# A mixture-of-experts router that works on batches of token tiles instead of one tile at a time

## The chip, the cores and the metric

The kernel runs on one core of a Trainium2 chip. The core has a matrix engine (TensorE, PE in the profile), a vector engine (VectorE, DVE), a scalar engine (ScalarE, ACT), GpSimd (POOL), and SP (SyncE), which here issues nearly all DMA transfers. The metric is the device time in microseconds (us), the median of several runs; lower is better.

## The reference

Two layers of a diffusion backbone work on 512 latent tokens and 256 context tokens of width 1024. Each layer mixes tokens in four groups of heads, projects the result back with w_out and adds it to the stream with a gate, and then runs a mixture of experts:

```python
def moe_ffn(h, wg, bg, we, be, w_gate, w_up, w_down):
    lg = hf @ wg + bg                                  # 4 groups
    pg = softmax(lg)
    g_sel = argmax(lg)
    p_sel = pg[g_sel]
    le = (hf @ we + be).reshape(T, 4, 8)               # 8 experts in each group
    top_v, top_i = top_k(le[g_sel], 2)
    wts = softmax(top_v) * p_sel
    eid = g_sel * 8 + top_i
    ...
    # for each expert e: the rows sent to it
    y = (silu(x @ w_gate[e]) * (x @ w_up[e])) @ w_down[e]
    # out[token] += weight * y
```

h is the normed and modulated stream: each row of x is scaled by the inverse root of its mean square, then by (1 + scale) and gain, and a shift is added. All of it is float32. Layer 0 routes 768 tokens, layer 1 only the 512 latent ones. There are 32 experts, each with 6 MB of weights.

## The kernel before

A tile here is 128 tokens. Layer 0 has nt = 6 tiles (four latent, two context), layer 1 has nt = 4. The code is written as a program in order; a scheduler then sets the order of the instructions on each engine, so instructions of neighbouring tiles may be interleaved on an engine, but each engine, and SP's queue of transfers, works strictly in the order that it was given.

**The end of the output projection.** For each of four column blocks c (256 columns) and each tile t, 24 matmuls (L1787; three products of high and low parts, eight each) fill a PSUM bank, VectorE multiplies it by the gate (L1790) and GpSimd adds it to the tile x1[t] (L1791). In the last block (c == 3) the router is woven in, LAG = 2 tiles behind.

**token_tile(t)** (L1751). SP stores x1[t] as the start of the accumulator (L1753). TensorE transposes the tile into PSUM in eight parts (L1757), ScalarE sums its squares and copies the transposed tile to hTt (L1759), and TensorE makes 36 logits from it (L1762, 16 instructions in the trace). row_rs (L1165) and small_rsqrt (L1149) turn the sum of squares into the row scale rs by nine small VectorE instructions (L1171, L1154, L1155, and L1158 and L1162 three times). VectorE scales the tile (L1768), GpSimd adds the shift (L1769), SP stores h2 (L1770). The logits are scaled and biased by L1772. At t == 0 and t == 4 new modulation rows are loaded first (bc_row, L1766); their buffers and PSUM's two-bank tags allow one set at a time.

**Router.tile(t, lg)** (L897) finds the group maximum, masks the other groups, finds the best and second-best expert by first_max (L886: a maximum, a mask times an index table, a minimum, a mask), and makes the two weights. It counts rows for the same expert in earlier tokens with two small matmuls (L922, L923), splits the weights into three bf16 parts (L926, L928), and for each of the two choices makes EV, a mask times six values (L932), the row's rank R (L933), and for two blocks of 64 slots a 0/1 selection S (L936), which a matmul adds into the tables L (L937). Where an operand is one number per row, these instructions take it as a scalar operand. Most scratch tags have two buffers.

**finish() and table()** (L940, L951) read L for each of the two blocks (L956) and make gather indices, scatter indices and weights, by about a dozen instructions on 32 columns a block.

**The experts.** moe() (L1057) gathers the rows of each expert from the stored h2 (L990, GpSimd), runs up (L1012) and down (L1039) projections and scatters the results (L1052). Expert weights come in chunks of 1 MB, six an expert, by fetch() (L1378), each held back until the fifth before it has landed (FLIGHT = 5). Some chunks are asked for early: FIRST = 12 in layer 0 and 16 in layer 1 ahead of the experts, of which 4 and 7 before the output projection (EARLY). Their places are those that other tiles have left: the sides of the output projection's weights, and in layer 1 also scratch of the router. The chunks up to the eighteenth wait for the second gather, "tokens before more weights".

Of the kernel before, what the change touches and what calls it, by code (L numbers as in the profile page):

```python
# [18 lines left out]
P = 128  # L19
# [165 lines left out]
def bcast(ap, *shape):  # L185
    return ap.to_broadcast(list(shape))
# [678 lines left out]
class Router:  # L865
# [20 lines left out]
    def first_max(self, v, w, iota, tag):  # L886

        E, nc = self.E, self.E.nc
        m, i = E.t(tag + "m", 1, bufs=2), E.t(tag + "i", 1, bufs=2)
        e = E.t(tag + "e", w, bufs=2)  # L890
        nc.vector.reduce_max(m, v, axis=AX)
        nc.vector.scalar_tensor_tensor(e, v, m, iota, op0=ALU.is_equal, op1=ALU.mult)  # L892
        nc.vector.tensor_reduce(i, e, axis=AX, op=ALU.min)
        nc.vector.tensor_scalar(e, iota, i, None, op0=ALU.is_equal)  # L894
        return e, m

    def tile(self, t, lg):  # L897

        E, nc = self.E, self.E.nc
        io4, io32 = E.c["miota"][:, :4], E.c["miota"][:, 4:36]  # L900
        G, gm = self.first_max(lg[:, :4], 4, io4, "rg")
        sm = E.t("rsm", 8, bufs=2)
        ex, lm = E.t("rex", 4, bufs=2), E.t("rlm", [4, 8], bufs=2)
        nc.vector.tensor_scalar(sm[:, 0:1], gm, -1.0, None, op0=ALU.mult)
        nc.scalar.activation(ex, lg[:, :4], AF.Exp, bias=sm[:, 0:1], accum_out=sm[:, 1:2])
        nc.vector.tensor_scalar(G, G, -1.0, 1.0e30, op0=ALU.add, op1=ALU.mult)
        nc.vector.tensor_tensor(lm, lg[:, 4:36].rearrange("p (g e) -> p g e", g=4), bcast(G.unsqueeze(2), P, 4, 8), op=ALU.add)
        lm = lm.rearrange("p g e -> p (g e)")
# [3 lines left out]
        nc.scalar.activation(sm[:, 2:3], v1, AF.Exp, scale=-1.0, bias=v2)  # L912
        nc.vector.scalar_tensor_tensor(sm[:, 3:4], sm[:, 2:3], 1.0, sm[:, 1:2], op0=ALU.add, op1=ALU.mult)
        w = sm[:, 4:6]
        nc.vector.reciprocal(w[:, 0:1], sm[:, 3:4])
        nc.vector.tensor_mul(w[:, 1:2], w[:, 0:1], sm[:, 2:3])

        Ab = E.t("rA", 32, BF16, bufs=2)
        nc.vector.tensor_add(Ab, E1, E2)
        nc.vector.tensor_add(self.seen[:, t + 1], self.seen[:, t], Ab)  # L920
        rk = E.p1()[:, :32]
        nc.tensor.matmul(rk, E.c["before_b"], Ab, start=True, stop=False, skip_group_check=True)  # L922
        nc.tensor.matmul(rk, E.c["ones_b"], self.seen[:, t], start=False, stop=True, skip_group_check=True)  # L923
        v = self.vals[:, :, t]
        for part in range(3):
            nc.vector.tensor_copy(v[:, :, 2 + part], w)  # L926
            if part < 2:
                nc.vector.tensor_sub(w, w, v[:, :, 2 + part])  # L928
        tmp = E.t("rtmp", 32, bufs=2)
        for k, Ek in enumerate((E1, E2)):  # L930
            R, EV = self.R[:, k, t:t + 1], self.EV[:, k, t]
            nc.vector.tensor_tensor(EV, bcast(Ek.unsqueeze(1), P, 6, 32), bcast(v[:, k].unsqueeze(2), P, 6, 32), op=ALU.mult)  # L932
            nc.vector.tensor_tensor_reduce(tmp, Ek, rk, 1.0, 0.0, op0=ALU.mult, op1=ALU.add, accum_out=R)  # L933
            for b in range(2):
                S = E.t("rS", 128, BF16, bufs=4)
                nc.vector.tensor_scalar(S, self.slots, float(b * NSLOT), R, op0=ALU.add, op1=ALU.is_equal)  # L936
                nc.tensor.matmul(self.L[:, b * 512:b * 512 + 192], S, EV.rearrange("p v e -> p (v e)"),  # L937
                                 start=(t == 0 and k == 0), stop=(t == self.nt - 1 and k == 1), skip_group_check=True)

    def finish(self):  # L940

        E, nc = self.E, self.E.nc
        tables = [self.table(self.L[:, b * 512:b * 512 + 192], 32, self.keep, f"s{b}") for b in range(2)]
        c = E.p1()[:, :32]
        nc.tensor.matmul(c, E.c["ones_b"], self.seen[:, self.nt], start=True, stop=True)
        nc.vector.tensor_copy(self.cnt, c)
        nc.vector.reduce_max(self.most, c, axis=AX)
        nc.vector.tensor_copy(self.top, self.most)
        return tables

    def table(self, L, ne, keep, tag):  # L951


        E, nc = self.E, self.E.nc
        Ls, f = E.t(tag + "Ls", [6, ne], bufs=1), E.t(tag + "f", [2, ne], bufs=1)
        nc.vector.tensor_copy(Ls, L.rearrange("p (v e) -> p v e", v=6))  # L956
        w = keep.t(tag + "w", [2, ne], F32, 1, P)
        gi, si = keep.t(tag + "gi", ne, I32, 1, P), keep.t(tag + "si", ne, I32, 1, P)
        pc = E.c["mpc"]
        nc.vector.scalar_tensor_tensor(f[:, 0], Ls[:, 1], 128.0, Ls[:, 0], op0=ALU.mult, op1=ALU.add)  # L960
        nc.vector.tensor_scalar(f[:, 0], f[:, 0], 2.0, pc[:, 0:1], op0=ALU.mult, op1=ALU.add)
        nc.vector.tensor_copy(gi, f[:, 0])
        nc.vector.tensor_scalar(f[:, 1], Ls[:, 5], -1.0, 1.0, op0=ALU.mult, op1=ALU.add)
        nc.vector.scalar_tensor_tensor(f[:, 1], f[:, 1], pc[:, 1:2], f[:, 0], op0=ALU.mult, op1=ALU.add)
        nc.vector.tensor_copy(si, f[:, 1])
        nc.vector.tensor_add(w[:, 0], Ls[:, 2], Ls[:, 3])
        nc.vector.tensor_add(w[:, 0], w[:, 0], Ls[:, 4])
        if self.nt * 128 > NLAT:
            nc.vector.scalar_tensor_tensor(w[:, 1], Ls[:, 1], NLAT / 128 - 0.5, w[:, 0], op0=ALU.is_gt, op1=ALU.mult)
            nc.vector.tensor_sub(w[:, 0], w[:, 0], w[:, 1])  # L970
        return gi, si, w

    def later(self, e, off):

        E, nc = self.E, self.E.nc
        L = E.p1()[:, :6]
        n = 2 * self.nt
        for i in range(n):
            k, t = i // self.nt, i % self.nt
            S = E.t("rS", 128, BF16, bufs=4)  # L980
            nc.vector.tensor_scalar(S, self.slots, off, self.R[:, k, t:t + 1], op0=ALU.add, op1=ALU.is_equal)
            nc.tensor.matmul(L, S, self.EV[:, k, t, :, e], start=(i == 0), stop=(i == n - 1), skip_group_check=True)
        return self.table(L, 1, E.cur, "sb")
# [181 lines left out]
def row_rs(E, x, tag):  # L1165

    nc = E.nc
    rs = E.t(tag, 1, bufs=2)
    junk = E.t(tag + "j", DM, BF16, bufs=1)
    nc.scalar.activation(junk, x, AF.Square, accum_out=rs)  # L1170
    nc.vector.tensor_scalar(rs, rs, 1.0 / DM, EPS, op0=ALU.mult, op1=ALU.add)  # L1171
    small_rsqrt(E, rs, tag)
    return rs


# [168 lines left out]
ARENA = 49536 - SIDE  # L1344
# [10 lines left out]
LAG = 2  # L1355
AHEAD = 1
# [41 lines left out]
def half_rows(a, t):  # L1398

    return a[t * 256:(t + 1) * 256].rearrange("(p a) c -> p (a c)", a=2)  # L1400


def trunk(tc, d, out):
# [7 lines left out]
    with ExitStack() as top:  # L1411
# [90 lines left out]
        for l in range(2):  # L1502
# [248 lines left out]
            def token_tile(t):  # L1751
# [15 lines left out]
                h2 = E.t("h2", DM, bufs=2)  # L1767
                nc.vector.scalar_tensor_tensor(h2, x1[t], rs, mod[0], op0=ALU.mult, op1=ALU.mult)  # L1768
                nc.gpsimd.tensor_add(h2, h2, mod[1])  # L1769
                nc.sync.dma_start(half_rows(h2d[l], t), h2)  # L1770
                lg = E.t("rlg", 36, bufs=2)
                nc.vector.scalar_tensor_tensor(lg, ps[:, :36], rs, cb[v], op0=ALU.mult, op1=ALU.add)  # L1772
                return lg

            mod, logits = [], []
            for c in range(4):
# [3 lines left out]
                for t in range(nt + LAG * (c == 3)):  # L1780
# [168 lines left out]
```

## Time and profile before

| | |
|---|---|
| median of 3 runs | 2420.07 us (2411.84 to 2425.87) |
| the profiled execution | 2419.79 us, its span 2418.0 us |
| granted TensorE clock, mean | 0.956 |
| TensorE busy | 84% of the span |
| VectorE busy | 41% |
| ScalarE busy | 24% |
| GpSimd busy | 22% |
| DMA from HBM | 554.17 MB, 244 GB/s over the span |
| first gathers | 812.19 us (layer 0) and 1911.46 us (layer 1) from the span's start |

The span runs from the first to the last instruction; the profiled execution's own time has 1.8 us around it. Shares of busy time are means over stages with different limits, so a change in one stage is read from rows of that stage. In the rows, PE is TensorE, DVE VectorE, ACT ScalarE, POOL GpSimd and SPq SP's queue; "out<-in" are the program's names; "arena" and "side" are the two pools of on-chip memory from which nearly all tiles come. A clock of 1.00 is 2.4 GHz, 0.50 is 1.2 GHz. A releaser behind "<-" is the work whose end let the waiting instruction go.

### The profile page before, as it was taken

How to read it: one execution, taken by the hardware profiler on the slowest of the kernel's cores; microseconds unless marked ns; L12 is line 12 of the kernel's file. 1: busy time of each engine (PE TensorE's matmuls, PEld its weight loads, DVE VectorE, ACT ScalarE, POOL GpSimd, SP SyncE). 2: the span in 40 equal slices, each digit the busy share in tenths (PEclk: the TensorE clock that was granted, in tenths of full speed). 3: DMA queues.
4: the chain of work that ended last, by engine and by line, in shares of the span. 5: the costliest groups of instructions: out<-in, count | busy, mean ns of one | idle time of the engine just before them, and what ended most of it. 6: DMA issues, size and time to landing. Idle time of an engine off the chain costs nothing. (4 is left out here: it accounts for less than half of the span.)

```text
span 2418.0 us, 32200 instructions
## 1 busy us (share of the span) xinstructions
PE 2039.0 (84%) x11540; PEld 1186.2 (49%) x11540; DVE 999.4 (41%) x2435; ACT 573.2 (24%) x1138; POOL 537.2 (22%) x429
## 2 busy tenths in 40 slices
PE   5789999999999598887777598999899598877775
PEld 1458778766688333322222386686669333222221
DVE  6751865537746522221112437645584511111110
ACT  4433431344622100000000234314352100000000
POOL 1653413211013122211111225131102221111111
PEclk9999999999998699999999799999999699999998
DMA  6434524202244899999999425420233899999996
GB/s 242 165 116 176 194 105 147 81 9 69 85 143 142 299 378 387 405 401 404 400 395 411 173 92 175 147 103 18 86 126 133 313 393 410 409 408 409 410 403 258
DMA packets 139311, 581.54 MB, mean 241 GB/s; under 512 B 23984, under 2 KB 47873, under 8 KB 88630
## 3 DMA queue, kind: packets, MB, share of 16 engines
q1 hardware_dynamic: 124054, 555.89, 59.5%
q0 software_dynamic: 15008, 22.36, 3.9%
q8 instruction: 152, 2.49, 0.4%
q14 instruction: 97, 0.79, 0.1%
HBM read 554.17 MB, written 36.80 MB: 244 GB/s over the span
## 5 line engine op out<-in xcount | busy, mean ns | idle before, releaser
L1012 PE MATMUL pb<-side,arena 128*64 128x512 f32 x1224 | 288.9, 604 | 45.9 <-DMA side<-in_w_moe 42.2
L1016 DVE COPY arena<-pb 128x512 f32<-128x512 f32 x67 | 46.3, 691 | 501.5 <-PE pb L1012 501.5
L1012 PE MATMUL pb<-arena 128*64 128x512 f32 x920 | 217.9, 605 | 41.8 <-DMA arena<-in_w_moe 38.2
L1028 ACT ACTIVATE arena<-pb 128x256 f32<-128x256 f32 x67 | 25.7, 383 | 902.9 <-PE pb L1025 902.9
L1276 POOL TENSOR_TENSOR wl<-side,wh 128x1024 fp32r<-128x1024 f32 x52 | 125.4, 2412 | 395.5 <-ACT wh L1275 267.1
L1012 PEld LDWEIGHTS pb<-side,arena 128*64 128x64 f32 x1224 | 81.4, 137 | 246.5 <-issue 126.4
L1300 PE MATMUL pw<-hh,wh 128*128 128x512 f32 (+1 forms) x720 | 168.6, 366 | 3.1 <-DVE arena L495 1.9
L1300 PE MATMUL pw<-hh,wl 128*128 128x512 f32 (+1 forms) x720 | 160.5, 358 | 0.0
L1043 DVE SCALAR_TENSOR_TENSOR arena<-pb,arena 128x512 f32<-128x512 f32 x67 | 50.3, 750 | 263.2 <-PE pb L1039 254.5
L1039 PE MATMUL pb<-side,arena 128*64 128x512 f32 x576 | 137.8, 617 | 24.9 <-DVE arena L1029 20.4
L1300 PE MATMUL pw<-hl,wh 128*128 128x512 f32 (+1 forms) x720 | 158.2, 355 | 0.0
L1012 PEld LDWEIGHTS pb<-arena 128*64 128x64 f32 x920 | 62.2, 138 | 190.8 <-issue 96.0
L1052 POOL DMA_INDIRECT acc<-arena x35 | 55.2, 1577 | 387.8 <-DVE arena L1047 338.5
L1300 PEld LDWEIGHTS pw<-hh,wh 128*128 128x128 f32 x720 | 117.8, 190 | 36.1 <-issue 14.4
L1039 PE MATMUL pb<-arena 128*64 128x512 f32 x496 | 115.5, 599 | 21.3 <-DVE arena L1029 20.8
L1300 PEld LDWEIGHTS pw<-hh,wl 128*128 128x128 f32 x720 | 117.9, 189 | 25.1 <-issue 9.9
L1300 PEld LDWEIGHTS pw<-hl,wh 128*128 128x128 f32 x720 | 117.4, 189 | 24.4 <-issue 8.7
L1052 POOL DMA_INDIRECT out_dram<-arena x32 | 50.9, 1590 | 311.4 <-DVE arena L1043 297.2
L990 POOL DMA_INDIRECT arena<-h2d,arena x67 | 69.8, 1042 | 187.5 <-issue 56.0
L1791 POOL TENSOR_TENSOR arena<-arena 128x256 f32<-128x256 f32 x40 | 31.2, 782 | 292.2 <-DVE arena L1790 278.2
L1025 PE MATMUL pb<-ident,arena 128*128 128x128 f32 x268 | 42.4, 280 | 55.4 <-DVE arena L1016 55.4
L1039 PEld LDWEIGHTS pb<-side,arena 128*64 128x64 f32 x576 | 39.0, 140 | 101.5 <-issue 60.8
(367 smaller groups left out, 3444.2 us busy)
## 6 DMA issues: line engine op xcount, KB each, us to landing
side<-in_w_moe SPq DMA_DIRECT2D x215, 1024.0 KB
arena<-in_w_moe SPq DMA_DIRECT2D x169, 1024.0 KB
arena<-in_w_ada SPq DMA_DIRECT2D x53, 512.0 KB
side<-in_w_in SPq DMA_DIRECT2D x52, 512.0 KB
side<-in_w_ada SPq DMA_DIRECT2D x43, 512.0 KB
arena<-in_w_out SPq DMA_DIRECT2D x16, 512.0 KB
arena<-in_x SPq DMA_DIRECT2D x12, 512.0 KB
spd<-arena SPq DMA_DIRECT2D x23, 256.0 KB
```

The lines of the kernel that those rows point to most:

```text
L990: E.gathered = nc.gpsimd.indirect_dma_start(out=xg, out_offset=None, in_=h2d, in_offset=bass.IndirectOffsetOnAxis(ap=gi, axis=0), **(dict( ...
L1012: nc.tensor.matmul(pg[64 * s:64 * s + 64], xT[:, j // 4, j % 4, :], W[j // 2][:, (j % 2) * 1024 + s * 512:(j % 2) * 1024 + s * 512 + 512], ...
L1016: nc.vector.tensor_copy(gu, pg)
L1025: nc.tensor.transpose(pt[:, c * 128:(c + 1) * 128], gu[:, c * 128:(c + 1) * 128], E.c["ident"])
L1028: nc.scalar.activation(hT, pv[:, :, 0, :], AF.Silu)
L1039: nc.tensor.matmul(pd[64 * s:64 * s + 64], hT[:, c, :], W[4 + c // 2][:, (c % 2) * 1024 + s * 512:(c % 2) * 1024 + s * 512 + 512], start=( ...
L1043: nc.vector.scalar_tensor_tensor(y, pd, w[0], g2[0], op0=ALU.mult, op1=ALU.mult)
L1052: E.nc.gpsimd.indirect_dma_start(out=acc, out_offset=bass.IndirectOffsetOnAxis(ap=si, axis=0), in_=y, in_offset=None, compute_op=ALU.add, ...
L1276: (nc.vector if k % 2 else nc.gpsimd).tensor_sub(lo, src, hi.bitcast(F32))
L1300: nc.tensor.matmul(ps[:, :n], w[:, j, :], h[:, j, a:a + n], start=(i == 0), stop=(i == 23))
L1791: nc.gpsimd.tensor_add(x1[t][:, cc], x1[t][:, cc], tmp)
```

## The change

The router works on batches of tiles: in layer 0 on tiles 0 to 3 and then on 4 and 5, in layer 1 on 0 and 1 and then on 2 and 3. token_tile(t, i) keeps the transposes, the sum of squares and the logits, which go to the i-th part of one PSUM bank. After a batch's last tile, token_batch(t0, n) makes the row scales of the n tiles together, the logits, then the n h2 tiles one after the other, and Router.tiles(t0, lg) does the routing with a further dimension of n. Operands of one number per row and tile are now broadcast along the free dimension, so several instructions with a scalar operand become a tensor_tensor, and some fused ones become two. Most scratch tags have one buffer that holds four tiles. finish() makes both tables by one call. The order of the code behind the batch's logits is row scales, logits, modulation rows, h2, routing.

```diff
     def first_max(self, v, w, iota, tag):
...
+        m, i = E.t(tag + "m", 4, bufs=1)[:, :n], E.t(tag + "i", 4, bufs=1)[:, :n]
+        e = E.t(tag + "e", [4, w], bufs=1)[:, :n]
+        wide = lambda a: bcast(a.unsqueeze(2), P, n, w)
+        row = bcast(iota.unsqueeze(1), P, n, w)
         nc.vector.reduce_max(m, v, axis=AX)
-        nc.vector.scalar_tensor_tensor(e, v, m, iota, op0=ALU.is_equal, op1=ALU.mult)
+        nc.vector.tensor_tensor(e, v, wide(m), op=ALU.is_equal)
+        nc.vector.tensor_tensor(e, e, row, op=ALU.mult)
         nc.vector.tensor_reduce(i, e, axis=AX, op=ALU.min)
-        nc.vector.tensor_scalar(e, iota, i, None, op0=ALU.is_equal)
+        nc.vector.tensor_tensor(e, row, wide(i), op=ALU.is_equal)
         return e, m
 
-    def tile(self, t, lg):
+    def tiles(self, t0, lg):
...
+        G, gm = self.first_max(lg[:, :, :4], 4, io4, "rg")
+        sm = E.t("rsm", [4, 4], bufs=2)[:, :, :n]
+        ex, lm = E.t("rex", [4, 4], bufs=2)[:, :n], E.t("rlm", [4, 32], bufs=1)[:, :n]
+        nc.vector.tensor_tensor(ex, lg[:, :, :4], bcast(gm.unsqueeze(2), P, n, 4), op=ALU.subtract)
+        nc.scalar.activation(ex, ex, AF.Exp)
         nc.vector.tensor_scalar(G, G, -1.0, 1.0e30, op0=ALU.add, op1=ALU.mult)
...
         E1, v1 = self.first_max(lm, 32, io32, "r1")
         nc.vector.scalar_tensor_tensor(lm, E1, -1.0e31, lm, op0=ALU.mult, op1=ALU.add)
         E2, v2 = self.first_max(lm, 32, io32, "r2")
...
+        nc.vector.tensor_sub(sm[:, 0], v2, v1)
+        nc.scalar.activation(sm[:, 0], sm[:, 0], AF.Exp)
+        Ab = E.t("rA", [4, 32], BF16, bufs=1)[:, :n]
         nc.vector.tensor_add(Ab, E1, E2)
...
+        rk = E.p1()[:, :n * 32].rearrange("p (n e) -> p n e", e=32)
+        for i in range(n):
+            nc.vector.tensor_add(self.seen[:, t0 + i + 1], self.seen[:, t0 + i], Ab[:, i])
+            nc.tensor.matmul(rk[:, i], E.c["before_b"], Ab[:, i], start=True, stop=False, skip_group_check=True)
+            nc.tensor.matmul(rk[:, i], E.c["ones_b"], self.seen[:, t0 + i], start=False, stop=True, skip_group_check=True)
+        nc.vector.tensor_reduce(sm[:, 1], ex, axis=AX, op=ALU.add)
...
         for k, Ek in enumerate((E1, E2)):
...
-            for b in range(2):
-                S = E.t("rS", 128, BF16, bufs=4)
-                nc.vector.tensor_scalar(S, self.slots, float(b * NSLOT), R, op0=ALU.add, op1=ALU.is_equal)
...
+            nc.vector.tensor_tensor(self.EV[:, k, tt], bcast(Ek.unsqueeze(2), P, n, 6, 32),
+                                    bcast(v[:, k].unsqueeze(3), P, n, 6, 32), op=ALU.mult)
+        for k, Ek in enumerate((E1, E2)):
+            nc.vector.tensor_tensor(Ek, Ek, rk, op=ALU.mult)
+            nc.vector.tensor_reduce(self.R[:, k, tt], Ek, axis=AX, op=ALU.add)
+        R1 = E.t("rR1", [2, 4], bufs=2)[:, :, :n]
+        nc.vector.tensor_scalar(R1, self.R[:, :, tt], -float(NSLOT), None, op0=ALU.add)
+        for k in range(2):
+            for b, R in enumerate((self.R[:, :, tt], R1)):
+                S = E.t("rS", [4, 128], BF16, bufs=2)[:, :n]
+                nc.vector.tensor_tensor(S, bcast(self.slots.unsqueeze(1), P, n, 128),
+                                        bcast(R[:, k].unsqueeze(2), P, n, 128), op=ALU.is_equal)
+                for i in range(n):
+                    nc.tensor.matmul(self.L[:, b * 512:b * 512 + 192], S[:, i],
...
     def finish(self):
...
-        tables = [self.table(self.L[:, b * 512:b * 512 + 192], 32, self.keep, f"s{b}") for b in range(2)]
+        gi, si, w = self.table(self.L.rearrange("p (b c) -> p b c", b=2)[:, :, :192], 2, 32, self.keep, "s")
...
-ARENA = 49536 - SIDE
+ARENA = 49664 - SIDE
...
+BATCHES = (((0, 4), (4, 2)), ((0, 2), (2, 2)))
...
-            def token_tile(t):
+            def token_tile(t, i):
...
-                rs = row_rs(E, x1[t], "rs2")
+                if i == 0:
+                    batch[:] = [E.p1()[:, :144].rearrange("p (n e) -> p n e", e=36), E.t("rs2", 4, bufs=2)]
+                nc.scalar.activation(E.t("xoj", DM, BF16, bufs=1), x1[t], AF.Square, accum_out=batch[1][:, i:i + 1])
                 nc.scalar.copy(hTt, pt.rearrange("p (j t) -> p j t", j=8))
...
+            def token_batch(t0, n):
+
+                v = t0 // 4
+                ps, rs = batch[0][:, :n], batch[1][:, :n]
+                nc.vector.tensor_scalar(rs, rs, 1.0 / DM, EPS, op0=ALU.mult, op1=ALU.add)
+                small_rsqrt(E, rs, "rs2", n)
+                lg = E.t("rlg", [4, 36], bufs=1)[:, :n]
+                nc.vector.tensor_tensor(lg, ps, bcast(rs.unsqueeze(2), P, n, 36), op=ALU.mult)
+                nc.vector.tensor_tensor(lg, lg, bcast(cb[v].unsqueeze(1), P, n, 36), op=ALU.add)
+                if t0 % 4 == 0:
                     n2 = E.load("h2", d[f"n2g{l}"], bufs=2)
                     mod[:] = [bc_row(v, 4, "rsc", 1), bc_row(v, 3, "rsh", 1)]
                     nc.vector.scalar_tensor_tensor(mod[0], mod[0], 1.0, n2, op0=ALU.add, op1=ALU.mult)
...
+                for i in range(n):
+                    h2 = E.t("h2", DM, bufs=2)
+                    nc.vector.scalar_tensor_tensor(h2, x1[t0 + i], rs[:, i:i + 1], mod[0], op0=ALU.mult, op1=ALU.mult)
+                    nc.gpsimd.tensor_add(h2, h2, mod[1])
+                    nc.sync.dma_start(half_rows(h2d[l], t0 + i), h2)
+                rt.tiles(t0, lg)
...
                     if c == 3 and t >= LAG:
-                        logits.append(token_tile(t - LAG))
-                        if t > LAG:
-                            rt.tile(t - LAG - 1, logits[t - LAG - 1])
-            rt.tile(nt - 1, logits[-1])
+                        t0, n = [b for b in batches if b[0] <= t - LAG][-1]
+                        token_tile(t - LAG, t - LAG - t0)
+                        if t - LAG == t0 + n - 1:
+                            token_batch(t0, n)
```

## Rows read from the trace of the kernel before

**Rows 1.** View by windows, both router stages: busy us (instructions), clock, DMA share, GB/s.

```profile
771.00:812.20 41.20, 23.77 (x132) 20.35 (x130) 36.72 (x228) 8.84 (x21) 7.74 (x5) 0.58 0.79 278
815.00:825.00 10.00, 6.32 (x18) 2.23 (x20) 0.00 (x0) 0.58 (x1) 3.90 (x4) 0.50 0.75 228
1877.00:1890.00 13.00, 6.21 (x30) 5.58 (x31) 12.90 (x67) 3.99 (x10) 3.09 (x2) 0.50 0.83 272
1890.00:1911.50 21.50, 12.32 (x59) 10.39 (x59) 14.64 (x119) 2.42 (x8) 2.38 (x2) 0.50 0.91 352
1911.50:1925.00 13.50, 7.65 (x22) 2.72 (x24) 0.13 (x2) 0.58 (x1) 4.93 (x5) 0.53 0.84 294
2025.00:2125.00 100.00, 83.25 (x392) 29.27 (x390) 13.04 (x21) 6.78 (x14) 18.42 (x14) 1.00 1.02 409
```

**Rows 2.** Timeline of SP's queue around both gathers: start, us, line, transfer, count.

```profile
799.29 3.08 SPq L1378 DMA_DIRECT2D side<-in_w_moe  x5
820.57 1.42 SPq L1378 DMA_DIRECT2D side<-in_w_moe  x2
...
1893.02 3.83 SPq L1378 DMA_DIRECT2D side<-in_w_moe  x5
1908.53 7.36 SPq L1378 DMA_DIRECT2D arena<-in_w_moe  x3
```

**Rows 3.** Waits of SP's queue, first stage, then second: total us, times, longest us.

```profile
SPq L1770 <- POOL arena L1769: 35.5, 6, 14.4
SPq L1378 <- DMA arena<-h2d,arena: 6.7, 1, 6.7
...
SPq L1378 <- DVE arena L932: 11.5, 1, 11.5
```

**Rows 4.** VectorE groups by form, first router stage: busy us, mean ns.

```profile
L1768 DVE SCALAR_TENSOR_TENSOR arena<-arena 128x1024 f32<-128x1024 f32 x6 | 7.7, 1280 | 0.2
L936 DVE TENSOR_SCALAR arena<-miota,arena 128x128 bf16<-128x128 f32 x24 | 6.3, 278 | 0.0
L892 DVE SCALAR_TENSOR_TENSOR arena<-arena,miota 128x4 f32<-128x4 f32 x6 | 5.4, 893 | 0.0
L932 DVE TENSOR_TENSOR arena<-arena 128x192 bf16<-128x192 f32 x12 | 4.3, 397 | 0.0
```

**Rows 5.** GpSimd group by form, same stage.

```profile
L1769 POOL TENSOR_TENSOR arena<-arena 128x1024 f32<-128x1024 f32 x6 | 14.2, 2365 | 28.7 <-DVE arena L1768 23.6 <-DVE arena L916 3.3 <-PE pa L1757 1.7
```

**Rows 6.** VectorE timeline: two dependent instructions of one tile.

```profile
760.11 0.19 DVE L907 TENSOR_TENSOR arena<-arena 128x32 f32<-128x32 f32 x1
760.34 0.19 DVE L891 TENSOR_REDUCE arena<-arena 128x1 f32<-128x32 f32 x1
```

**Rows 7.** View by windows, VectorE alone.

```profile
747.25:809.40 62.15, 57.11 (x290) 0.69 0.63 226
801.04:809.35 8.31, 8.22 (x68) 0.50 1.02 382
1864.57:1908.70 44.13, 36.70 (x193) 0.63 0.75 282
```

**Rows 8.** TensorE timeline, first stage: end of a projection, transposes, one tile's logits.

```profile
755.02 1.12 PE L1787 MATMUL pw<-woh,ol 128*128 128x256 f32 x8
755.98 1.03 PE L1757 MATMUL pa<-ident,arena 128*128 128x128 f32 x8
760.86 3.63 PE L1762 MATMUL pb<-arena 128*128 128x36 f32 x16 [2.65 <-ACT arena L1759]
```

**Rows 9.** Timeline from the tables' first instruction to the first gather, first layer.

```profile
809.87 0.62 DVE L956 COPY arena<-pa 128x192 f32<-128x192 f32 x2 [0.34 <-PE pa L937]
...
812.19 1.25 POOL L990 DMA_INDIRECT arena<-h2d,arena  x1 [13.30 <-DVE arena L948]
```

**Rows 10.** Timeline, second layer: one tile's last projection to its row scale.

```profile
1862.12 0.42 DVE L1790 TENSOR_TENSOR arena<-pw,arena 128x256 f32<-128x256 f32 x1 [2.46 <-PE pw L1787]
...
1864.57 0.15 DVE L1171 TENSOR_SCALAR arena<-arena 128x1 f32<-128x1 f32 x1 [2.03 <-ACT arena L1170]
```

More of the change, by code (lines that the diff above doesn't have):

```diff
@@ L906, in tile @@
         nc.vector.tensor_scalar(G, G, -1.0, 1.0e30, op0=ALU.add, op1=ALU.mult)
[L907 to L908 removed]
+        nc.vector.tensor_tensor(lm.rearrange("p n (g e) -> p n g e", g=4),
+                                lg[:, :, 4:36].rearrange("p n (g e) -> p n g e", g=4),
+                                bcast(G.unsqueeze(3), P, n, 4, 8), op=ALU.add)
@@ new lines, in tiles @@
+        for k, Ek in enumerate((E1, E2)):
[10 more added lines that the diff above has]
+                    nc.tensor.matmul(self.L[:, b * 512:b * 512 + 192], S[:, i],
+                                     self.EV[:, k, t0 + i].rearrange("p v e -> p (v e)"),
+                                     start=(t0 + i == 0 and k == 0), stop=(t0 + i == self.nt - 1 and k == 1),
+                                     skip_group_check=True)
@@ L948, in finish, with table @@
         nc.vector.tensor_copy(self.top, self.most)
-        return tables
-    def table(self, L, ne, keep, tag):
+        return [(gi[:, b], si[:, b], w[:, :, b]) for b in range(2)]
+    def table(self, L, nb, ne, keep, tag):
         E, nc = self.E, self.E.nc
[L955 to L958, printed above, removed]
+        Ls, f = E.t(tag + "Ls", [nb, 6, ne], bufs=1), E.t(tag + "f", [2, nb, ne], bufs=1)
+        nc.vector.tensor_copy(Ls.rearrange("p b v e -> p b (v e)"), L)
+        w = keep.t(tag + "w", [2, nb, ne], F32, 1, P)
+        gi, si = keep.t(tag + "gi", [nb, ne], I32, 1, P), keep.t(tag + "si", [nb, ne], I32, 1, P)
         pc = E.c["mpc"]
-        nc.vector.scalar_tensor_tensor(f[:, 0], Ls[:, 1], 128.0, Ls[:, 0], op0=ALU.mult, op1=ALU.add)
+        nc.vector.scalar_tensor_tensor(f[:, 0], Ls[:, :, 1], 128.0, Ls[:, :, 0], op0=ALU.mult, op1=ALU.add)
         nc.vector.tensor_scalar(f[:, 0], f[:, 0], 2.0, pc[:, 0:1], op0=ALU.mult, op1=ALU.add)
         nc.vector.tensor_copy(gi, f[:, 0])
-        nc.vector.tensor_scalar(f[:, 1], Ls[:, 5], -1.0, 1.0, op0=ALU.mult, op1=ALU.add)
+        nc.vector.tensor_scalar(f[:, 1], Ls[:, :, 5], -1.0, 1.0, op0=ALU.mult, op1=ALU.add)
         nc.vector.scalar_tensor_tensor(f[:, 1], f[:, 1], pc[:, 1:2], f[:, 0], op0=ALU.mult, op1=ALU.add)
         nc.vector.tensor_copy(si, f[:, 1])
-        nc.vector.tensor_add(w[:, 0], Ls[:, 2], Ls[:, 3])
-        nc.vector.tensor_add(w[:, 0], w[:, 0], Ls[:, 4])
+        nc.vector.tensor_add(w[:, 0], Ls[:, :, 2], Ls[:, :, 3])
+        nc.vector.tensor_add(w[:, 0], w[:, 0], Ls[:, :, 4])
         if self.nt * 128 > NLAT:
-            nc.vector.scalar_tensor_tensor(w[:, 1], Ls[:, 1], NLAT / 128 - 0.5, w[:, 0], op0=ALU.is_gt, op1=ALU.mult)
+            nc.vector.scalar_tensor_tensor(w[:, 1], Ls[:, :, 1], NLAT / 128 - 0.5, w[:, 0], op0=ALU.is_gt, op1=ALU.mult)
             nc.vector.tensor_sub(w[:, 0], w[:, 0], w[:, 1])
@@ L1766, in token_tile @@
                     nc.vector.scalar_tensor_tensor(mod[0], mod[0], 1.0, n2, op0=ALU.add, op1=ALU.mult)
[L1767 to L1775, printed above, removed]
+                for i in range(n):
[4 more added lines that the diff above has]
+                rt.tiles(t0, lg)
+            mod, batch = [], []
+            batches = BATCHES[l]
             for c in range(4):
```

56 lines of the change are left out of this document (15 added, 41 removed).

## The prediction

> **What bounds the kernel now.** The place to begin is the window view of an expert phase: in 100 us of it the DMA engines are busy throughout at 409 GB/s while TensorE is only 83% busy (2025 to 2125) [rows 1]. So each expert phase lasts as long as its 192 weight chunks of 1 MB take, counted from the moment the stream runs without holes. The router matters only through that moment. The reader should see three holes ahead of it: DMA share 0.79 from 771 to 812.2 and 0.75 in the ten us after that in layer 0; 0.83, 0.91 and 0.84 from 1877 to 1925 in layer 1 [rows 1]. As idle time that is 41.2 x 0.21 + 10 x 0.25 = 11.2 us and 13 x 0.17 + 21.5 x 0.09 + 13.5 x 0.16 = 6.3 us. Together, 17.5 us, they are about all that a sooner router can win.
>
> Next, SP's queue and its waits say what ends each hole. In layer 0 five weight chunks leave at 799.29, behind h2 stores for which SP stood still (14.4 us once, for GpSimd's addition); the next leave at 820.57, after a 6.7 us wait for the gathered tokens [rows 2, 3]. That is 8.4 us behind the first gather at 812.19 [rows 9]. In layer 1 the same five leave at 1893.02, and the ninth of its nine at 1908.53 after an 11.5 us wait for VectorE, because its place in the arena is the router's own scratch [rows 2, 3]. So the end of the router releases weights directly.
>
> Then, what sets the end of the router: VectorE alone has 57.1 us of work in 62.2 us, and 36.7 in 44.1 [rows 7]. TensorE waits for it by way of ScalarE (2.65 us before one tile's logits) and falls to the low clock (3.63 us for 16 small matmuls) [rows 8]; its mean clock is 0.58 after 771 [rows 1].
>
> **The change, on VectorE.** Counting the code, a tile now issues 44 small VectorE instructions (9 for the row scale, 1 logits, 34 in tile()). A batch of n tiles issues 55 + n: first_max grows from 4 to 5, the row scale from 9 to 12, logits from 1 to 2. Layer 0 goes from 264 to 59 + 57 = 116, layer 1 from 176 to 114. But the work removed was cheap: tiles were interleaved, and 68 instructions of two tiles took 8.31 us, 0.122 each [rows 7]. One tile's dependent instructions start 0.23 us apart [rows 6]. In the change most scratch buffers of a batch have one copy, so the second batch can't pass its first expert maximum until the first has used its E1. I therefore cost the new router as a chain at 0.23 us a step, plus 1.1 ns for each element beyond 32 ((1.28 - 0.19) us over 992 elements, L1768 against L907 [rows 4, 6]).
>
> For n = 2: 6 steps on groups at 0.20; 16 on 32 experts at 0.25; the count matmuls with nine weight instructions above them 1.4; two EV products of 384 elements 0.9; rank and offset 0.9; four selections of 256 elements at 0.33 (1.3). Sum 9.7 us. For n = 4 the same steps: 1.3 + 5.4 + 1.6 + 1.8 + 1.2 + 2.4 = 13.7, say 13.5 as a few overlap. Row scale: 12 x 0.19 = 2.3. Bounds: fully interleaved like the old code (0.122 each plus the longer operands, 1.1 ns x 4,224 and 1,408 elements), row scale included, 11.8 and 8.5 in place of 15.8 and 12.0; with nothing of the second batch in the gaps, 2.0 more a layer. I take the chain, since the single copies force it.
>
> The selections and products with a broadcast operand don't occur in this form before; L932, a product with two broadcast operands (0.40 us for 192 elements), and L936 (0.28 for 128) are nearest [rows 4]. The Trainium skill's page "VectorE: DVE Perf Modes", section "The perf-mode tier table", gives fp32 tensor_scalar twice the rate of tensor_tensor, which speaks against swapping L936's form for the broadcast one; at the faster rate the four selections would take some 1.1 us less for n = 4 and 0.6 for n = 2. L936's 0.28 us against 0.30 by the slope hardly tells the two apart.
>
> **What stays.** Each tile still needs its h2 multiplication (1.28 us) and GpSimd's addition behind it (2.37) [rows 4, 5]. While that addition runs, one VectorE instruction stands: L892 on four elements averages 0.89 us [rows 4]. So a tile costs VectorE up to 3.65 us, before and after, here in a row of four.
>
> **What moves.** VectorE's router work may start only when a whole batch has its squares. In layer 1 a tile's scale begins 2.45 us after its last projection is read out [rows 10]; a projection takes 3 x 0.96 = 2.88 [rows 8], so the scale of tiles 0 and 1 begins at 1862.12 + 2.88 + 2.45 = 1867.5 in place of 1864.6. In layer 0 the fourth tile's projection ends at 756.0 [rows 8] and the scale begins at 758.6 in place of 747.3 [rows 7]: 11 us in which VectorE has little to do. That is the price of a batch of four. On TensorE, ScalarE's copies no longer queue behind an exponential of each tile, so batch 0's logits come near 773 (two projections and three tiles of transposes and logits after 756, at the high clock) to 780 (at the low one).
>
> **Layer 0 in order.** Scale 758.6 to 760.9; four h2 tiles, 14.6 plus 0.8 for h2's two buffers, to 776.3; batch 0's chain to 789.8 (logits are there); the context rows' product and two h2 tiles, 1.2 + 7.3, to 798.3; batch 1's chain less its first 2.0 us, done in gaps, to 806.0. Before: 809.35 [rows 7]. **Layer 1:** scale to 1869.8, two h2 tiles to 1877.1, chain to 1886.8, two h2 tiles to 1894.1, 7.7 more to 1901.8; before 1908.7 [rows 7].
>
> The joint tables take one copy and the three instructions up to the first gather, about 1.5 us in place of 2.3 [rows 9]: 0.8 a layer, bounds 0 and 1.2. First gathers so come 4.2 and 7.8 us sooner.
>
> **What of it reaches the end.** Layer 0: all 4.2, since the five chunks in front need 5.2 MB / 409 GB/s = 12.8 us and are in by 812 to 815, ahead of 820.6 - 4.2. Layer 1: the eight chunks before the ninth leave hardly sooner, as they stand behind the same stores; what the earlier ninth chunk can fill is the idle share from 1890 to 1925, 4.1 us. Sum 8.3 us. The profiled execution took 2419.8, the median of the runs is 2420.1: **2411.5 us**. The shorter instruction list, PSUM held by a batch, and 128 more arena columns I cost at nothing: TensorE and SP have idle time beside them; were the PSUM bank to hold up tile 4's logits, it would cost 3.6 us of TensorE, still ahead of batch 1's turn on VectorE.
>
> **Rivals.** (1) *Throughput, not the chain, decides.* Gaps are filled as now: layer 0 then needs 11.8 + 8.5 + 23.9 from 758.6, ending at 802.8, layer 1 17.0 + 14.6 + 0.8 from 1867.5, ending at 1899.9; with the tables 7.3 and 9.6 us, and if SP lets the side chunks go as much sooner, all of it arrives: 2403. For it: VectorE held 0.122 us an instruction [rows 7]. Against: the single copies. The same page, section "Rules for kernel authors", advises cutting the number of VectorE operations because each pays its pipe's flush; rows 7 against rows 6 show that independent ones here pay about half.
>
> (2) *No gain arrives.* The context's two modulation rows can be loaded only after batch 0's last addition (776.3), behind up to five weight chunks (12.8 us); h2 of tiles 4 and 5 and the last store then end where they do now, and the gather needs every store. 2419.
>
> (3) *The weight stream waits behind the stores; slower.* SP takes its transfers in order, and stores now come in pairs at the end of a batch. If all eight side chunks queue behind the last store, they need 20.5 us after it. That decides from a last store at 800 in layer 0 (820.6 - 20.5) and 1888 in layer 1 (1908.5 - 20.5). With stores at 806, after batch 1's chain, and at 1894: 6.3 + 6.4 us later; with layer 1's behind its chain too, 20 in all: 2432 to 2440, I take 2434. For it: SP already lost 14.4 us so [rows 3]. Against: three chunks slipped between stores before.
>
> **Chances.** Forecast 0.42, (1) 0.30, (2) 0.14, (3) 0.14. A measurement here tells 0.5% from no change, 12.1 us, so faster means below 2408 and slower above 2432. Faster: nine tenths of (1) and a sixth of the forecast, 0.34. Slower: most of (3), 0.13. Same: 0.53. Range: from 2396, rival (1) less the half-spread of the runs shown, to 2428, half of (3); the forecast's own is 2404 to 2418. Some 0.16 lies outside.
>
> **What would show it.** Right: about 116 and 114 small instructions, VectorE's steps 0.2 to 0.3 us apart within a batch, first gathers 4 and 8 us sooner counted from the last projection, and the same 409 GB/s afterwards. Wrong: steps near 0.12 (rival 1); the last h2 store no sooner (2); a longer line of weight issues straight after it, and DMA share under 0.7 ahead of the gather (3). A clock that stays high up to the experts would break the forecast upwards too.

## The result, and the profile after

The changed kernel takes 2438.30 us (median of 7 runs, 2435.16 to 2443.64) where the kernel before takes 2418.11 beside it: ratio 1.0096, 95% interval 1.0081 to 1.0111. It is 20 us above the kernel before; forecast were 2411.5 us and a range up to 2428. The profiled execution has a span of 2434.0 us against 2418.0.

I cut each span at two marks of each layer: the readout of tile 0's last projection block (L1790 before, L1809 after; 744.79 and 1862.12 before, 741.83 and 1863.94 after) and the first gather. The changed kernel reached the first mark 2.96 us sooner, which I put down to chance: in the runs of this document that mark lies between 738.1 and 747.3. From there, layer 0 takes 1122.1 us in place of 1117.3 up to layer 1's mark (first gather after 70.5 in place of 67.4), and layer 1 takes 570.1 in place of 555.9 (first gather after 63.5 in place of 49.3): -2.96 + 4.8 + 14.2 = 16.0, the whole difference. Behind layer 1's gather both kernels need the same 506.5 us. Of the 19.0 us lost behind the first mark, 14.2 are thus lost in the router stage of layer 1, and 4.8 between layer 0's mark and layer 1's.

The first view is that of VectorE alone in the two stretches from mark to gather (us, busy and instructions, clock, DMA share, GB/s), of the changed kernel; the second the same of the kernel before.

```profile
741.83:812.35 70.52, 43.05 (x143) 0.74 0.57 221
1863.94:1927.44 63.50, 34.14 (x134) 0.62 0.56 215
```

```profile
744.79:812.19 67.40, 59.99 (x310) 0.69 0.63 229
1862.12:1911.46 49.34, 39.55 (x212) 0.64 0.72 268
```

The change does what it says: VectorE has 16.9 us less work in layer 0 and 5.4 less in layer 1. But the stretches became longer, so VectorE idles 27.5 us in place of 7.4, and 29.4 in place of 9.8. The Trainium skill's page "VectorE: DVE Perf Modes", section "Rules for kernel authors", advises fewer VectorE operations; VectorE's busy time here, 22.3 us less in the two stretches, agrees with it; the kernel's time does not follow.

The view by windows of the changed kernel (columns as in [rows 1]) shows where the weight stream lost its time: a DMA share of 0.56 from 1877 to 1890 where [rows 1] have 0.83, 0.35 from 1911.5 to 1927.4 where [rows 1], with the gather already done at 1911.46, have 0.84, and the same 410 GB/s once it runs.

```profile
771.00:812.40 41.40, 15.84 (x101) 11.95 (x101) 34.14 (x122) 3.82 (x8) 8.65 (x5) 0.60 0.75 286
815.00:825.00 10.00, 4.72 (x14) 1.87 (x16) 0.00 (x0) 0.59 (x1) 3.91 (x4) 0.50 0.72 212
1877.00:1890.00 13.00, 5.78 (x28) 5.42 (x28) 6.32 (x19) 2.05 (x3) 5.43 (x3) 0.63 0.56 202
1890.00:1911.50 21.50, 9.26 (x46) 8.00 (x45) 11.08 (x42) 2.44 (x4) 3.27 (x2) 0.50 0.88 342
1911.50:1927.40 15.90, 5.90 (x29) 4.00 (x28) 10.75 (x57) 0.41 (x2) 0.00 (x0) 0.50 0.35 133
2025.00:2125.00 100.00, 84.87 (x404) 30.44 (x406) 13.86 (x23) 7.76 (x16) 18.44 (x14) 1.00 1.02 410
```

TensorE's timeline in layer 1 says why VectorE idles (L1764 transposes, L1770 logits, L924 and L925 rank matmuls, L950 table matmuls).

```profile
1882.14 3.63 PE L1770 MATMUL pb<-arena 128*128 128x36 f32 x16 [2.99 <-ACT arena L1768]
1897.29 0.18 PE L924 MATMUL pb<-arena,before_b 128*128 128x32 bf16 x1 [11.52 <-DVE arena L920]
...
1900.32 0.50 PE L950 MATMUL pa<-arena 128*128 128x192 bf16 x2 [2.64 <-DVE arena L947]
1900.62 0.64 PE L1764 MATMUL pa<-ident,arena 128*128 128x128 f32 x2
...
1904.65 3.63 PE L1770 MATMUL pb<-arena 128*128 128x36 f32 x16 [1.16 <-ACT arena L1768]
1908.09 1.95 PE L1764 MATMUL pa<-ident,arena 128*128 128x128 f32 x8
1911.19 3.63 PE L1770 MATMUL pb<-arena 128*128 128x36 f32 x16 [1.16 <-ACT arena L1768]
```

Tiles 0 and 1 have their logits at 1885.8. Then TensorE stands for 11.52 us in front of batch 0's rank matmuls, which wait for VectorE; the transposes of tiles 2 and 3, whose x1 was done at 1871.7 and 1880.0, stand behind them in its queue. Their logits follow one after the other at the low clock (3.63 us for 16 matmuls). VectorE's timeline is the other half.

```profile
1885.80 0.23 DVE L1780 TENSOR_TENSOR arena<-pb,arena 128x72 f32<-128x72 f32 x1 [2.58 <-PE pb L1770]
...
1888.68 2.30 DVE L894 TENSOR_TENSOR arena<-arena 128x8 f32<-128x8 f32 x1
...
1891.02 2.27 DVE L895 TENSOR_TENSOR arena<-arena,miota 128x8 f32<-128x8 f32 x1
...
1914.86 0.23 DVE L1780 TENSOR_TENSOR arena<-pb,arena 128x72 f32<-128x72 f32 x1 [12.82 <-PE pb L1770]
...
1923.12 1.45 DVE L947 TENSOR_TENSOR arena<-miota,arena 128x256 bf16<-128x256 f32 x3
```

The two steps of 2.3 us stand while GpSimd adds two h2 tiles (1887.58 to 1893.27). Batch 1's chain runs from 1914.86 to 1924.57, after a wait of 12.82 us. In layer 0 the same wait is 3.67 us. Batch 0's own logits are late as well; the chain of waits shows by what.

```profile
1873.72 4.55 POOL arena L1789 x2
1878.27 1.01 issue
1879.28 0.73 POOL arena L1810
1880.06 0.94 issue
1881.19 0.91 ACT arena L1768
1882.14 3.64 PE pb L1770 x16
```

GpSimd adds two h2 tiles (L1789) ahead of tile 3's last projection addition (L1810). ScalarE's square of tile 3 (L1767) waits for that, and stands ahead of the copy of tile 1 (L1768), for which the logits wait; ScalarE's timeline has the two.

```profile
1880.04 1.06 ACT L1767 ACTIVATE arena<-arena 128x1024 bf16<-128x1024 f32 x1 [6.29 <-POOL arena L1810]
...
1881.09 0.99 ACT L1768 COPY arena<-pa 128x1024 f32<-128x1024 f32 x1
```

### The profile page after: what moved, and what is told of

The parts are those of the page before. It is cut to its first block, busy times and chain, and to the rows that moved or that the text cites. A ratio compares the mean times of both kernels' runs of the same rounds, so it can differ in the third digit from the quotient of the medians.

```text
span 2434.0 us, 31922 instructions
## 1 busy us (share of the span) xinstructions
PE 2034.9 (84%) x11540; PEld 1178.2 (48%) x11540; DVE 974.7 (40%) x2185; ACT 569.0 (23%) x1116; POOL 540.9 (22%) x429
## 5 line engine op out<-in xcount | busy, mean ns | idle before, releaser
L1006 POOL DMA_INDIRECT arena<-h2d,arena x67 | 69.9, 1043 | 204.1 <-issue 60.6
L1810 POOL TENSOR_TENSOR arena<-arena 128x256 f32<-128x256 f32 x40 | 33.3, 831 | 296.7 <-DVE arena L1809 189.6
```

The lines of the kernel that those rows point to most:

```text
L1006: E.gathered = nc.gpsimd.indirect_dma_start(out=xg, out_offset=None, in_=h2d, in_offset=bass.IndirectOffsetOnAxis(ap=gi, axis=0), **(dict( ...
L1810: nc.gpsimd.tensor_add(x1[t][:, cc], x1[t][:, cc], tmp)
```

## The experiments

The experiments change order or batch sizes only, except for two (layer 0 tiles, and best of all) in which layer 0 has the code of the kernel before. A to D are stretches of each one's profiled execution in us: A from layer 0's mark to its first gather, B to layer 1's mark, C from there to the first gather, D to the end. The same program gave 70.5 and 73.8 for A (changed kernel, one batch), and 552.6, 553.8, 552.9, 556.6 for D (the four runs whose layer 1 is the same), so a single stretch is good to about 2 us either way.

| kernel | median us | ratio to before, 95% interval | A | B | C | D |
|---|---|---|---|---|---|---|
| before | 2412.3 to 2418.1 in the groups | 1 | 67.4 | 1117.3 | 49.3 | 555.9 |
| changed | 2438.30 | 1.0096, 1.0081 to 1.0111 | 70.5 | 1122.1 | 63.5 | 570.1 |
| logits first | 2421.39 | 1.0012, 0.9993 to 1.0031 | 69.6 | 1119.9 | 48.7 | 557.5 |
| ScalarE and GpSimd order | 2436.45 | 1.0071, 1.0050 to 1.0093 | 74.2 | 1124.9 | 58.6 | 567.3 |
| both orders | 2418.51 | 1.0001, 0.9986 to 1.0015 | 68.1 | 1119.0 | 44.6 | 556.6 |
| layer 1 one batch | 2430.95 | 1.0061, 1.0041 to 1.0082 | 73.8 | 1123.7 | 50.5 | 565.9 |
| weights before stores | 2415.44 | 1.0014, 0.9996 to 1.0033 | 70.0 | 1118.1 | 44.7 | 552.6 |
| one batch, all orders | 2419.58 | 1.0013, 0.9999 to 1.0027 | 70.0 | 1118.4 | 46.5 | 557.4 |
| single tiles | 2428.72 | 1.0066, 1.0042 to 1.0090 | 73.6 | 1121.2 | 54.1 | 563.1 |
| layer 0 three pairs | 2419.30 | 1.0007, 0.9991 to 1.0023 | 69.3 | 1120.0 | 44.9 | 553.8 |
| layer 0 tiles, layer 1 batches | 2409.71 | 0.9982, 0.9969 to 0.9994 | 66.1 | 1115.1 | 45.2 | 552.9 |
| before, weights first | 2411.63 | 0.9986, 0.9972 to 1.0000 | 65.6 | 1111.7 | 49.7 | 556.3 |
| best of all | 2412.75 | 0.9997, 0.9979 to 1.0015 | 65.2 | 1111.5 | 45.8 | 556.6 |

**Logits first.** The routing of a batch is written behind the next batch's token tiles (DEFER is 2: two tiles after the batch's last).

```diff
-                rt.tiles(t0, lg)
+                routed.append((t0, lg))
...
                         token_tile(t - LAG, t - LAG - t0)
+                        if routed and t - LAG - routed[0][0] - TAIL(batches, routed[0][0]) == DEFER[l]:
+                            rt.tiles(*routed.pop(0))
                         if t - LAG == t0 + n - 1:
                             token_batch(t0, n)
+            for r in routed:
+                rt.tiles(*r)
```

> Program order alone is changed: the routing of a batch is written behind the next batch's token tiles, in both layers; nothing is left out. Theory Q (TensorE's queue: the second batch's transposes and logits stand behind the first batch's rank and table matmuls, and VectorE waits 12.8 us for them in layer 1 and 3.7 in layer 0): the logits of all tiles stand ahead of the first rank matmul. In layer 1 the last logits end near 1899, the rank matmuls wait 1.7 us for them, the second batch follows the first at once, and the first gather comes near 1916 in place of 1927.4; in layer 0 about 4 us sooner. Together 15 us under the changed kernel: 2423, 0.2% over the kernel before. Theory S (SP's stores and the weights behind them set the time, the router's end does not): last h2 stores stay at 795 and 1894, and so does the time, 2438. Theory C (VectorE's chain itself is longer than costed): no wait of 12.8 us was needed to explain the loss, and the time stays within 3 us of 2438.

Measured: 1.0012, so 0.84% or some 20 us under the changed kernel by the two ratios, 17 by the medians (forecast 15), and C falls from 63.5 to 48.7. TensorE's timeline has all logits ahead of the first rank matmul, and VectorE's wait for batch 1's logits is down to 1.17 us:

```profile
1889.19 3.47 PE L1772 MATMUL pb<-arena 128*128 128x36 f32 x16
1893.82 3.63 PE L1772 MATMUL pb<-arena 128*128 128x36 f32 x16 [1.16 <-ACT arena L1770]
1900.64 0.21 PE L924 MATMUL pb<-arena,before_b 128*128 128x32 bf16 x1 [3.20 <-DVE arena L920]
```

```profile
1897.48 0.23 DVE L1782 TENSOR_TENSOR arena<-pb,arena 128x72 f32<-128x72 f32 x1 [1.17 <-PE pb L1772]
```

SP's queue keeps its order: the last stores, and seven side chunks behind them. First this run, then the changed kernel.

```profile
1892.88 2.64 SPq L1792 DMA_DIRECT2D h2d<-arena  x2
1895.57 9.31 SPq L1386 DMA_DIRECT2D side<-in_w_moe  x7
```

```profile
1890.99 2.62 SPq L1790 DMA_DIRECT2D h2d<-arena  x2
1893.66 9.81 SPq L1384 DMA_DIRECT2D side<-in_w_moe  x7
```

VectorE's steps for batch 1 now fill batch 0's gaps (up to the first of these, 31 us behind layer 1's mark, VectorE, GpSimd and SP keep the changed kernel's order). Theory Q holds: most of the loss was TensorE's queue. Theory S falls as the cause, since from layer 1's mark the stores and the seven chunks behind them leave within 0.4 us of the changed kernel's (26.7 and 29.4 us in place of 27.1 and 29.7) while the time falls. Theory C falls too.

**ScalarE and GpSimd order.** E.after(late, early) puts one instruction behind another in its engine's order, and does nothing else.

```diff
+    def after(self, late, early):
+        self.tc.add_manual_dep(late.ins, early.ins.name, ...
...
+                if t >= 2:
+                    E.after(sq, copies[t - 2])
...
-                    nc.gpsimd.tensor_add(h2, h2, mod[1])
+                    E.after(nc.gpsimd.tensor_add(h2, h2, mod[1]), last[0])
```

> Order alone is changed, nothing is left out: GpSimd's h2 additions come behind the last tile's projection addition, and ScalarE's square of tile t behind its copy of tile t-2. Theory W (the first batch's logits are late because GpSimd's two h2 additions, 5.6 us, stand ahead of the last tile's addition, and so the square of tile 3 ahead of the copy of tile 1): the first batch's logits in layer 1 are ready near 1883.5 in place of 1885.8, all behind them moves as much, and the time falls by 3 to 4 us to about 2434.5. Rival: h2 itself is what VectorE's router waits for (two VectorE steps of 2.3 us each stand while GpSimd adds); then the later additions push the routing back as much as the logits come sooner, and the time is 2438 to 2441. Theory Q alone: the second batch still stands behind the first, VectorE's wait for it stays 12 to 13 us.

Measured: 1.0071, under the changed kernel by 6 us by the ratios, whose intervals just overlap, and by 2 by the medians. In layer 1 batch 0's logits come 15.4 us behind the mark in place of 21.9, and C falls by 4.9. The second wait is untouched, as Q alone said:

```profile
1883.51 0.23 DVE L1786 TENSOR_TENSOR arena<-pb,arena 128x72 f32<-128x72 f32 x1 [3.59 <-PE pb L1776]
1914.13 0.23 DVE L1786 TENSOR_TENSOR arena<-pb,arena 128x72 f32<-128x72 f32 x1 [12.82 <-PE pb L1776]
```

In layer 0 A is 3.7 us longer, but that isn't shown to be the edit: batch 1's logits there ran at the low clock (3.63 us a tile, 1.98 in the changed kernel), as in the run with one batch, whose layer 0 is the changed kernel's and has an A of 73.8. Theory W is right for layer 1 by the logits and by C; by the time alone it is not clear of the noise.

**Both orders.** The two edits together.

> The two edits of the order together (all logits ahead of the first rank matmul; h2 additions behind the last projection addition; square of tile t behind the copy of tile t-2); nothing is left out. Theories Q and W both: 15 and 3.5 us off, about 2419.5, the time of the kernel before. Q alone: 2423. S: 2438.

Measured: 1.0001, the time of the kernel before, 23 us under the changed kernel by the ratios. The two waits explain the loss. C is 44.6, 4.8 us under the kernel before; D is not shorter. The weight stream has a hole ahead of each gather, which may be where that goes (windows of this run):

```profile
800.00:810.00 10.00, 0.65 (x5) 0.29 (x5) 9.92 (x19) 0.00 (x0) 5.62 (x2) 0.50 0.47 187
1890.00:1900.00 10.00, 1.64 (x10) 0.57 (x10) 9.95 (x32) 0.21 (x1) 4.68 (x2) 0.50 0.49 162
```

**Layer 1 one batch.** `BATCHES = (((0, 4), (4, 2)), ((0, 4),))`, program order as in the change.

> Layer 1 routes its four tiles as one batch, layer 0 as in the changed kernel; nothing is left out. With one batch no transposes stand behind another batch's rank matmuls, and the chain is one of 13.5 us in place of two of 9.7. Theory Q: logits complete near 1897 to 1899, gather near 1914 in place of 1927.4, so 13 us less than the changed kernel: 2425. Theory S: the stores are no sooner, 2438. Theory C (VectorE's chain sets it): 19.4 - 13.5 = 6 us less, 2432.

Measured: 1.0061, some 8 us under the changed kernel; C is 13.0 us shorter, as Q said, but D only 4.2: the last h2 stores left SP at 1901.55 (two, 3.82 us), ten us later than in the changed kernel, and five side chunks behind them. So C alone doesn't set the end. That SP's order takes part of it back is argued from these times; the run with one batch and all orders, below, bears on it. Q and S each explain a part.

**Weights before stores.** Both orders, and SP's:

```diff
             wts.fetch(FIRST[l])
+            for t in range(nt - 2, nt):
+                E.after(stores[t], wts.loads[(11, 14)[l]])
```

> The version with both orders, and on SP the last two h2 stores of a layer now stand behind the eight side weight chunks in place of ahead of them; nothing is left out. Theory S (what the better order won does not arrive because the side chunks wait on SP for the last h2 stores: DMA share 0.49 from 1890 to 1900 and 0.47 from 800 to 810): layer 1's hole of about 5 us fills, share there 0.9 or more, 2413.5; layer 0's chunks ahead of the gather are a fixed number, so its hole only moves. Rival: the first gather sets the stream by itself, and the last store, now 3 to 5 us later, holds it back: 2418.5 to 2422.

Measured: 1.0014, not to be told from the run before it by time. The hole in layer 1 filled (second line), the one in layer 0 moved behind the gather (first and third):

```profile
800.00:810.00 10.00, 2.24 (x10) 0.64 (x9) 8.30 (x31) 0.00 (x0) 2.09 (x1) 0.50 0.88 357
1890.00:1900.00 10.00, 3.08 (x15) 0.94 (x15) 9.58 (x49) 0.20 (x1) 0.00 (x0) 0.50 1.01 408
810.00:820.00 10.00, 0.52 (x3) 0.55 (x4) 0.00 (x0) 0.00 (x0) 5.01 (x5) 0.50 0.54 160
```

D is 4 us shorter in this profile, which is within twice its scatter. The rival has a part too: the gathers start 2.2 us (layer 0) and 0.8 us (layer 1) behind the tables' last instruction, in place of 0.3 and 0.4 in the changed kernel. The stores that now leave later would explain it; in the run with one batch and all orders the trace names them as what layer 1's gather waited for last. Whether the order pays stays open.

**One batch, all orders**, layer 1 as a batch of four with the three orders.

> Layer 1 as one batch of four, with the orders of the run before it on ScalarE, GpSimd and SP, and layer 0 as in it; nothing is left out. One chain of 13.5 us in place of two of 9.7, but all four h2 multiplications and additions, 14.6 us, stand between the row scale and the chain. Theory: routing starts near 1899 and the gather comes near 1915, 4 us behind two batches in order; 2417. Rival, the chain's 6 us saved decide: 2409.

Measured: 1.0013. C is 46.5, 1.8 us behind two batches; the rival's 2409 did not come. A longer batch wins nothing over two in order. Against one batch in program order, C is 4.0 us shorter and D 8.5, so about 4.5 us came behind the gather, where theory S has them.

**Single tiles.** `BATCHES` of (t, 1) and `DEFER = (1, 1)`.

> The changed kernel's instruction forms and single-copy scratch, but batches of one tile, each routed one tile later as in the kernel before; joint tables kept; nothing is left out. Theory C (single copies make each tile a dependent chain, about 8.8 us with n = 1): layer 0 needs 6 x 8.8 + 22 = 75 us of VectorE from 744.6, gather 11 us later than before; layer 1 36 + 14.6 = 50, 7 later; 2436. Rival (VectorE's throughput, 0.12 us an instruction, decides and neighbouring tiles still interleave): 57 small instructions in place of 44 add 1.6 us a tile, 2424 to 2434.

Measured: 2428.72, in the rival's range and 7 us under theory C. Windows of VectorE, from mark to gather:

```profile
738.42:811.98 73.56, 65.51 (x345) 0.70 0.60 222
1859.65:1913.79 54.14, 42.84 (x232) 0.64 0.68 253
```

VectorE is busy 89% of layer 0's stretch: neighbouring tiles do interleave with one copy of the scratch. The forms without the batches cost 6.2 us in A and 4.8 in C against the kernel before; against that C two batches with their logits first have 5.4 us less, and with both orders, of which the second has nothing to do with batches, 9.6.

**Layer 0 three pairs**, otherwise as weights before stores.

> As the first run of this group, but layer 0 routes three batches of two in place of four and two; nothing is left out. Theory (a batch of four is paid for by VectorE's 11 us with little to do while its squares and logits come): the first chain runs in that time, the gather in layer 0 comes 3 us sooner, 2410. Rival (three chains of 9.7 us against 13.5 and 9.7): the gather is 3 to 6 us later, 2417 to 2420.

Measured: 1.0007; A 69.3 against 70.0. Neither the theory's 3 us nor the rival's 3 to 6. The waiting of a batch of four and the third chain may pay each other; that isn't shown.

**Layer 0 tiles, layer 1 batches**, and **before, weights first** (the kernel before with the last diff alone).

> Layer 0 routes tile by tile with the code of the kernel before (joint tables kept), layer 1 in two batches with all three orders of the run with weights before stores; nothing is left out. Theory (layer 1's batches in that order end 3 us sooner than the kernel before, 552.6 against 555.9 us from the layer's last block to the end, and layer 0's batches cost 1 us): ratio to before 0.9986, 2412.5. Rival (those 3 us are chance of one execution): ratio 1.000 or above.

> The kernel before with one change of SP's order: the last two h2 stores of a layer behind the eight side chunks; nothing is left out. If the order of SP alone gives what the run with weights before stores won, the ratio is 0.9986; since the kernel before already had three chunks between its stores and a share of 0.90 there, I expect no more than 1 us: 0.9995.

Measured: 0.9982 and 0.9986. The first is under the kernel before by 0.18% (interval 0.06 to 0.31) and 28 us under the changed one. As the best of eleven versions it may be flattered by the choice. The second is 3.4 us under (interval 0 to 7), where I expected no more than 1; the interval holds both. Its B is 5.6 us shorter and its D the same. In layer 0 the kernel before has DMA shares of 0.68 from 780 to 790 and 0.49 from 790 to 800, ahead of its last stores; with the weights first that hole is filled, but one of 0.28 stands from 805 to 815, where the kernel before has 1.00. Layer 0's last gather comes 1.0 us sooner from the mark and its last scatter 3.4 us (598.8 in place of 602.2); the rest of the 5.6 us falls in work that the edit leaves alone. So it isn't shown that the filled hole won them.

**Best of all**: the former of the two, with the stores behind the weights in layer 0 too.

> Layer 0 tile by tile and layer 1 in two batches, as before, and now the last two h2 stores stand behind the eight side chunks in layer 0 as well; nothing is left out. If the order of SP's queue won its time in layer 0 (1111.7 against 1117.3 us from that layer's last block to the next's in the profiles) and the batches of layer 1 theirs in layer 1 (552.9 against 555.9), the two add: ratio 0.9968, 2408. Rival (both gains are the same holes of the weight stream, and do not add): 0.9983.

Measured: 0.9997, 0.9979 to 1.0015. B was 1111.5, D 556.6 in this profile, though its layer 1 is that of the run with 552.9. The gains did not add within what 12 runs can tell; the version with 0.9982 stays the best one shown.

## Why the prediction was wrong

**The step that failed** is the schedule of layer 1, "scale to 1869.8, two h2 tiles to 1877.1, chain to 1886.8, two h2 tiles to 1894.1, 7.7 more to 1901.8", and the remark that a bank holding up tile 4's logits would cost "3.6 us of TensorE, still ahead of batch 1's turn on VectorE". It has no row for TensorE between the batches: it takes each batch's logits as there when VectorE comes to them, and puts the wait for batch 1's at nothing. What TensorE has queued ahead of them was not asked. From the mark, the forecast has the last selection at 1901.8 - 1862.12 = 39.7 us, measured 1924.57 - 1863.94 = 60.6. The 20.9 us between are:

- 6.1 us: batch 0's chain and the four h2 tiles are through at 38.1 (1902.04) in place of 32.0 (39.7 less batch 1's 7.7), because batch 0's logits are read 21.9 us behind the mark. The text let ScalarE's copies run freely ("no longer queue behind an exponential"); they queued behind squares that waited for GpSimd. Shown by the second experiment: with batch 0's logits at 15.4 us, its chain and the four h2 tiles are through at 33.2.
- 12.8 us: batch 1's logits behind batch 0's rank and table matmuls. Shown by the first.
- 2.0 us: nothing of batch 1 done in batch 0's gaps, since its logits were not there.

So the forecast's 8.3 us of gain became a loss of 20. The gather of layer 1 came 14.2 us later from its mark than before, in place of 7.8 sooner, and the end of the span came as much later from that mark.

**What held.** The row scale began 5.34 us behind the mark (forecast 5.4), a chain of n = 2 took 9.71 us (9.7), its dependent steps stood 0.25 apart, an h2 tile cost 3.5 us (3.65), and the stream ran at 410 GB/s.

**What was mis-sized.** The chain of four took 11.4 us without the h2 work inside it (13.5). The joint tables won nothing: 2.28 us from first instruction to gather in layer 1 (1925.16 to 1927.44), 2.34 in layer 0, against 2.32 [rows 9]; in layer 1 of the changed kernel the gather starts 0.40 us after the table's last instruction, not after the index, and so it does in the runs with logits first, both orders and single tiles; why it waits for all was not tried. In layer 0 batch 0's routing began at 778.88, 37.1 us behind the mark in place of 31.5: the four h2 multiplications did not stand "in a row": in VectorE's order the second stood behind the readout of tile 4 (761.10), the third behind that of tile 5 (767.69), and the fourth behind batch 0's logits (775.02). And "the single copies force it" is wrong as a reason: single tiles interleaved with the same copies.

**The rivals.** (3) gave 2434 to the measured 2438, and its sign was there: seven chunks behind the last stores. But the loss went when TensorE's order changed and SP's did not, so its number was near by luck, by another cause. Its own sum is a little off as well: from its marks, 800.1 and 1888.0, stores at 806 and 1894 are 5.9 and 6.0 us late, not 6.3 and 6.4. Its mechanism shows at about 4.5 us with one batch in layer 1, and nowhere else clear of the scatter. (2)'s late modulation rows did not set the end: the context's product ran at 788.52, inside batch 0's chain. (1)'s throughput needs logits that are there; with both orders they are, and layer 1's gather comes 44.6 us behind the mark where (1), with 9.6 us won, had 49.3 - 9.6 = 39.7.

## What to carry to other kernels

Batching a chain that runs between two engines can take away the interleaving that hid the other engine's latency: for each engine in the loop, write down what its in-order queue holds ahead of the next batch's first input, not only the work saved on the busiest one. Produce the inputs of all batches ahead of the first batch's dependent matmuls; here that order alone gave back 17 of the 20 us lost by the medians. When an intermediate milestone moves and the end doesn't, look at the queue that feeds the next bound (SP's stores ahead of weights here) before calling the gain lost, and count its holes behind the milestone too: here one that was filled came back behind the gather, and the time did not clearly fall.

## What the runs showed of the hardware

TensorE's clock after a wait was not the same in two executions of the same instructions. Layer 0's second batch has the same instructions in the same order in the changed kernel and in the run with one batch in layer 1. In the first, its logits took 1.98 us a tile, at a granted clock of 0.84 from 790 to 800; in the second 3.63, at 0.50:

```profile
793.65 1.98 PE L1770 MATMUL pb<-arena 128*128 128x36 f32 x16
```

```profile
791.94 3.63 PE L1770 MATMUL pb<-arena 128*128 128x36 f32 x16
```

A differs by 3.2 us between the two. TensorE had stood 9.4 us in front of the rank matmuls in both, and came back at 0.50 (1.2 GHz) in both. Then both did the same table matmuls and transposes, with no wait over 0.3 us (from 788.59 and from 786.87); behind these the first was granted 0.87 from 793 to 794 and 1.00 (2.4 GHz) up to 800, the second 0.50 up to 812. Since the instructions up to there are the same, such a stage is not to be judged by one profile.

Independent small VectorE instructions go well below the 0.122 us of [rows 7]: in the run with single tiles those from 1882.07 to 1883.36 start 0.06 to 0.13 us apart, while dependent ones of the changed kernel (64 elements) stay at 0.25 or 0.26.
